# The odd layer's input projection by Strassen's algorithm, with its weight differences made in the even stage

## The chip, the cores and the metric

The kernel runs on one core of a Trainium2 chip. The metric is the device time of one execution in microseconds (us). The engines are PE (TensorE, matmuls), DVE (VectorE), ACT (ScalarE), POOL (GpSimd) and SP (which issues transfers only); each works through its own instructions in order, and each of SP, ACT and POOL can issue transfers.

## The reference

An inference step of a two-layer decoder trunk on a prompt of 2048 tokens and 64 sample tokens (8 sequences of 8), with a model width of 1024, all in fp32. Layer 0 ("even") has one input projection for two mixers: a causal pooling mixer and differential attention. Layer 1 ("odd") is gated linear attention (GLA):

```python
def odd_layer(x, s0, w_in, w_ga, w_gb, b_g, norm_w, w_out, ln_g, ln_b):
    q, k, v, g = jnp.split(x @ w_in, ODD_SPLITS, axis=-1)
    log_a = jax.nn.log_sigmoid(((x @ w_ga) @ w_gb + b_g)) / GLA_TAU
    ...
    o, s_end = gla_chunked(q, k, v, log_a, s0)
    o = rms_norm(o, norm_w).reshape(b, t, ODD_OUT_IN) * jax.nn.silu(g)
    y = layer_norm(DN_ALPHA * x + o @ w_out, ln_g, ln_b)
```

`w_in` of the odd layer has 1024 rows and 3072 columns: q and k with 512 columns each, v and the gate g with 1024 each. The change is about the product `x @ w_in` of this layer.

## The kernel before, in words

**Three products for one.** An fp32 matrix product is made from matmuls in fp32r, a form of lower precision: each operand is split into a high part, rounded, and a low part, the rest (`split`, L40 to L48: the high part by ACT or DVE, the low part on L48 by DVE), and `mm3` (L51 to L56) adds hi x hi, hi x lo and lo x hi in PSUM on three lines. A tensor's tile is 128 partitions wide; "k" counts the eight blocks of 128 of the width.

**Stages.** The even projection goes to about 547 us, attention with its fills to 1215, the odd projection from 1215.3 to 1804.7, and GLA with its output projection from there to the end. A tile scheduler sets the order on each engine from the program and its dependencies; memory that two pools share in turn adds waits (a later pool's tile waits for the last use of what lay there).

**The even projection already runs by Strassen's algorithm, one level**: for each set of 1024 tokens (2 sets) and each group of 1024 weight columns (3 groups), the product of two 2x2 matrices of blocks (x in quarters a11 to a22, weights in quarters b11 to b22, each block 512 x 512) is made of seven block products instead of eight (`fast`). They need sums of x parts (`XParts`, names s1 to s4) and differences of weight quarters (t1 to t4). Only set 0's first group is made plainly. `WParts` makes the differences once on the chip and puts them into DRAM; for the groups 1 and 2 in wide pieces (`make_wide`), for group 0 in pieces of 256 columns with four quarters in the single set of tiles of a pool, `comb`:

```python
with self.tc.issue_after(self.last.ins):
    for x in QUARTERS:
        b.append(pool.tile([128, n], F32, tag=x, name=f"{self.pre}m{x}{g}_{c}"))
        nc.gpsimd.dma_start(b[-1], self.at(g, x)[:, c:c + n])
for x, v in differences(nc, *b).items():
    nc.gpsimd.dma_start(self.t[g][x][:, c:c + n], v)
```

These are four loads (L386), four DVE differences (L336 to L339) and four stores (L388) a piece, all transfers on POOL's queue. The profile calls the tiles pmb and the differences' tensors pt; a wide piece is pn. `run` in `project_even` lets one more piece follow every second step of a product.

**Attention** goes head by head over 16 tiles of 128 tokens: scores (sc, in PSUM), exponentials (e), transposes (tp to aT), the product with the values (po) in the one bank of pool `apso`, and the result oq, which ACT copies from po and which is multiplied with a gate (sga, loaded by SP). oq and sga lie in a pool `arp`, opened once the even projection has closed its pools. `weave` puts fills between: the out projection of the pooling mixer (`out_pool`: products zp, with results zx, stored to z by POOL, and operands zh and zl split from zr by POOL or ACT) beside head 0, the samples' attention beside head 1, and the out projection of attention beside heads 2 and 3.

**The odd projection** (`Odd`, `project_odd`) keeps all its x resident, in hi and lo parts (`XSplit`), in the token chunks `CH` of 512, 512, 512, 256 and 320; the last holds the 64 sample tokens. q and k (products qm) come with weights as the stationary side, by 128 columns and chunk; v and the gate (vt) by tiles of 128 tokens. Each is a plain product: three matmuls for each of eight k. The forget gate (ga, gz, the scan to cb) runs beside q and k. 24 weight units of 128 x 1024 are loaded by SP into a ring of two (raw) and split to wk; v leaves through ACT's queue, q, k and cb through SP's, the gate through POOL's. Beside its last 5 token tiles, GLA's first chunks (`inside`) and four of the eight out weights are got ready; the other four follow, and then SP, DVE and the other engines pass a branch (L1420) that picks one of two forms of GLA. The loads of GLA's gates (gsg, gcb) stand behind it.

Of the kernel before, what the change touches and what calls it, by code (L numbers as in the profile page):

```python
# [26 lines left out]


CH = [(0, 512), (512, 512), (1024, 512), (1536, 256), (1792, 320)]
# [43 lines left out]
class XSplit:  # L73


    def __init__(self, tc, pools, raws, src, pre):
        self.tc, self.pools, self.raws, self.src, self.pre = tc, pools, raws, src, pre
        self.hi, self.lo = {}, {}

    def place(self, c, pool=None):  # L80
        pool = pool or self.pools[c]
        for z, part in (("h", self.hi), ("l", self.lo)):
            part[c] = pool.tile([128, 8, CH[c][1]], F32R, name=f"{self.pre}{z}{c}")

    def load(self, c, pool=None, before=None):

        nc = self.tc.nc
        t0, n = CH[c]
        if c not in self.hi:
            self.place(c, pool)  # L90
        h, l = self.hi[c], self.lo[c]
        for k in range(0, 8, 2):
            if before:
                before(k)
            raw = self.raws[(k // 2) % len(self.raws)]
            r = raw.tile([128, 2, n], F32, tag="raw", name=f"{self.pre}r{c}_{k}")
            load = nc.sync.dma_start(r, self.src[k:k + 2, :, t0:t0 + n].rearrange("k p t -> p k t"))
            split(nc, r, h[:, k:k + 2, :], l[:, k:k + 2, :], "act" if k % 4 or before else "dve")
        return load

    def tok(self, t0, n):
        for c, (c0, cn) in enumerate(CH):
            if c0 <= t0 < c0 + cn:
                o = t0 - c0
                return (lambda k: self.hi[c][:, k, o:o + n]), (lambda k: self.lo[c][:, k, o:o + n])

    def both(self, t, t0, n):

        c, o = next((c, t0 - c0) for c, (c0, cn) in enumerate(CH) if c0 <= t0 < c0 + cn)
        self.tc.nc.vector.tensor_copy(t[:, :, 0:n], self.hi[c][:, :, o:o + n])  # L110
        self.tc.nc.vector.tensor_copy(t[:, :, n:2 * n], self.lo[c][:, :, o:o + n])
        return lambda k: t[:, k, :]


# [32 lines left out]

class XParts:
# [14 lines left out]
    def sums(self, h):  # L163

        nc = self.tc.nc
        for x, y, op, z in (("s3", "a11", ALU.subtract, "a21"), ("s1", "a21", ALU.add, "a22"),
                            ("s2", "s1", ALU.subtract, "a11"), ("s4", "a12", ALU.subtract, "s2")):
            if x == "s1":
# [261 lines left out]
def layers(tc, d):  # L430
# [6 lines left out]
    with ExitStack() as left:  # L437
# [11 lines left out]
        for m, j in project_even(tc, d, dr, W, slot, psf):  # L449
# [26 lines left out]
    with ExitStack() as left:  # L476
# [4 lines left out]
        O = Odd(tc, d, odd, keep, A.ident)  # L481
# [13 lines left out]
    fill_banks.close()  # L495
# [4 lines left out]
def project_even(tc, d, dr, W, slot, psf):  # L500
# [4 lines left out]
    with ExitStack() as own:  # L505
# [7 lines left out]
        P = WParts(tc, dr, d["w0_q"], "p")  # L513
# [832 lines left out]
class Odd:  # L1346


    def __init__(self, tc, d, ctx, keep, ident):
        self.tc, self.d, self.ctx, self.ident = tc, d, ctx, ident  # L1350
# [4 lines left out]
        self.W = Weights(tc, self.raw, self.place, 200)  # L1355

# [3 lines left out]
    def first_weights(self):  # L1360
        self.w_first = [self.W.fm(self.d["w1_fm"][j]) for j in range(2)]

    def start(self):

        self.xq, self.p1 = ExitStack(), ExitStack()
        rq = self.pool(self.xq, "p1rq", 1, side="right")
        self.ps = self.pool(self.p1, "p1ps", 6, space=PSUM)
        self.X = XSplit(self.tc, {}, [self.raw, self.raw, rq], self.d["y0T"], "y")
        for c in range(2):
            self.load_right(c)  # L1370
        self.w_first += [self.W.fm(self.d["w1_fm"][j]) for j in (2, 3)]

    def load_right(self, c):
        self.X.load(c, self.pool(self.xq, f"p1xq{c}", 1, side="right"))

    def run(self):
        tc, d, ctx = self.tc, self.d, self.ctx
        nc = tc.nc
        cst = self.pool(ctx, "p1c", 1)
        ident = self.ident  # L1380
        steep = cst.tile([1, 32], I32, name="steep")[:, 0:1]
        self.load_right(2)
        xp = self.pool(self.p1, "p1x", 1)
        ev = self.pool(self.p1, "p1e", 10)

        def slot(name, n=512, dt=F32):
            return ev.tile([128, 512], dt, tag="g", name=name)[:, :n]

        last = project_odd(tc, d, self, cst, xp, slot, ident, steep)
        self.xq.close()  # L1390

        gw = self.pool(ctx, "gw", 4, side="right")
        gl = self.pool(ctx, "gl", 1, side="right")
        G = Gla(tc, d, ident, self.raw, gl)
        W = Weights(tc, self.raw, places(gw), 300)

        def bank(name):
            return self.ps.tile([128, 512], F32, tag="mm", name=name)

        def early():  # L1400
            for i in range(2):
                G.load(i, G.first + ("v1",))
            for k in range(4):
                G.w.append(W.unit(d["w1_out"][k]))
# [923 lines left out]
```

## Time and profile before

| | us |
|---|---|
| runs | 2173.31, 2176.49, 2186.42; median 2176.49 |
| profiled execution | 2179.26, its span 2177.5 |
| even projection, 0 to 547 | PE busy 525.6 |
| attention and fills, 547 to 1215.3 | 668.3, PE busy 604.9 |
| odd projection, 1215.3 to 1804.7 | 589.4, PE busy 586.9, DVE 165.4, ACT 115.9, POOL 69.8 |
| GLA and output, 1804.7 to 2177.5 | 372.8, PE busy 333.0 |

The mean granted clock of PE was 0.983. A row of instructions in the trace has the start, the duration, the engine, the line, the operation, the tile written and the tiles read, and the shape. In lists by line stand the count, the busy time with the mean in ns, and the idle time of the engine before them with what ended it. Buffer numbers are left out of names.

### The profile page before, as it was taken

The numbers are of one execution on the slowest core, as the hardware profiler recorded it, in microseconds if no ns is written. First come the engines' busy times: TensorE is split into PE (matmuls) and PEld (weight loads), VectorE is DVE, ScalarE is ACT, GpSimd is POOL, SyncE is SP. The second block draws the span as 40 slices with busy tenths as digits, with TensorE's granted clock in tenths as the row PEclk, the third lists the DMA queues.
The fourth block names the chain that finished last, engine by engine and source line by source line (L and its number), as shares of the span: only waits on it lengthen the run. The fifth ranks groups of instructions, "written<-read, shape, count | busy, mean of one in ns | idle before, by whom it ended". The sixth has DMA issues, their size and how long they took to land. (4 is left out here: it accounts for less than half of the span.)

```text
span 2177.5 us, 31247 instructions
## 1 busy us (share of the span) xinstructions
PE 2050.4 (94%) x11153; PEld 1688.1 (78%) x11153; DVE 1337.1 (61%) x2592; ACT 823.9 (38%) x1610; POOL 805.1 (37%) x975
## 2 busy tenths in 40 slices
PE   8999999999999999798888899999999997999997
PEld 7778788877788777587777688888888886778776
DVE  7698665656867666988676554710110127898894
ACT  4245442445533556654645212301111134333341
POOL 2345324125645423766443200000004343645554
PEclk9999999999999999999999999999999998999999
DMA  8877766268855797633322452311221237455422
GB/s 287 285 239 242 240 197 213 82 134 245 271 168 164 223 308 226 212 108 126 102 66 78 148 181 91 120 65 49 85 84 54 97 131 222 155 170 165 171 91 75
DMA packets 201064, 346.71 MB, mean 159 GB/s; under 512 B 26034, under 2 KB 108338, under 8 KB 200898
## 3 DMA queue, kind: packets, MB, share of 16 engines
q1 hardware_dynamic: 143282, 219.96, 32.9%
q0 software_dynamic: 33408, 104.47, 13.6%
q10 hardware_dynamic: 24208, 20.19, 2.8%
q8 instruction: 90, 1.47, 0.3%
q14 instruction: 76, 0.62, 0.1%
HBM read 229.56 MB, written 114.96 MB: 158 GB/s over the span
## 5 line engine op out<-in xcount | busy, mean ns | idle before, releaser
L1561 POOL TENSOR_TENSOR ve<-ve,nw 128x512 f32<-128x512 f32 (+1 forms) x34 | 44.8, 1320 | 473.2 <-ACT ve L1560 473.1
L1069 ACT ACTIVATE e<-sc,nm 128x896 f32<-128x896 f32 (+11 forms) x192 | 165.0, 865 | 121.5 <-DVE nm L1067 82.9
L56 PE MATMUL vt<-wk,yl 128*128 128x512 f32 x512 | 199.9, 391 | 0.0
L55 PE MATMUL vt<-wk,yh 128*128 128x512 f32 x512 | 199.7, 390 | 0.0
L54 PE MATMUL vt<-wk,yh 128*128 128x512 f32 x512 | 197.1, 391 | 0.0
L1054 DVE TENSOR_REDUCE nm<-sc 128x1 f32<-128x768 f32 (+7 forms) x160 | 156.7, 991 | 30.5 <-PE sc L1050 18.3
L48 DVE TENSOR_TENSOR wl<-wr,wh 128x1024 fp32r<-128x1024 f32 (+1 forms) x93 | 112.4, 1213 | 87.8 <-ACT wh L43 87.6
L47 DVE CAST wk<-wr 128x1024 fp32r<-128x1024 f32 x14 | 10.5, 751 | 251.8 <-PE vt L64 250.4
L1049 PE MATMUL sc<-kst,qh 128*128 128x512 f32 (+9 forms) x352 | 134.6, 385 | 29.4 <-ACT e L1069 27.3
L1094 PE MATMUL po<-vt,aT 128*128 128x128 f32 x1088 | 153.1, 280 | 3.5 <-ACT aT L1106 2.1
L1094 PEld LDWEIGHTS po<-vt,aT 128*128 128x128 f32 x1088 | 137.8, 194 | 10.2 <-ACT aT L1106 2.4
L43 ACT ACTIVATE wh<-wr 128x1024 fp32r<-128x1024 f32 (+1 forms) x86 | 88.9, 1038 | 129.2 <-PE f L55 64.2
L1106 ACT ACTIVATE aT<-tp 128x512 f32<-128x512 f32 (+3 forms) x160 | 85.6, 535 | 100.3 <-PE tp L1101 99.8
L1050 PE MATMUL sc<-kst,ql 128*128 128x512 f32 (+9 forms) x352 | 123.0, 352 | 0.0
L54 PE MATMUL qm<-yh,wk 128*128 128x512 f32 (+2 forms) x320 | 113.7, 356 | 5.4 <-DVE yh L47 4.8
L55 PE MATMUL qm<-yl,wk 128*128 128x512 f32 (+2 forms) x320 | 113.9, 356 | 0.0
L56 PE MATMUL qm<-yh,wk 128*128 128x512 f32 (+2 forms) x320 | 113.7, 355 | 0.0
L55 PEld LDWEIGHTS vt<-wk,yh 128*128 128x128 f32 x512 | 96.2, 188 | 20.5
L54 PEld LDWEIGHTS vt<-wk,yh 128*128 128x128 f32 x512 | 96.2, 188 | 20.5
L56 PEld LDWEIGHTS vt<-wk,yl 128*128 128x128 f32 x512 | 96.2, 188 | 20.5
L1049 PEld LDWEIGHTS sc<-kst,qh 128*128 128x128 f32 x352 | 68.3, 194 | 50.0 <-ACT e L1069 39.7
L1101 PE MATMUL tp<-ident,e 128*128 128x128 f32 x544 | 91.3, 282 | 12.8 <-ACT aT L1106 10.2
(646 smaller groups left out, 5799.6 us busy)
## 6 DMA issues: line engine op xcount, KB each, us to landing
wr<-pt SPq DMA_DIRECT2D x40, 512.0 KB, 6.4
wr<-in_w_q SPq DMA_DIRECT2D x37, 512.0 KB, 4.9
sk<-in_cachek SPq DMA_DIRECT2D x64, 256.0 KB, 3.8
sv<-in_cachev SPq DMA_DIRECT2D x64, 256.0 KB, 4.7
pt<-pn POOLq DMA_DIRECT2D x32, 256.0 KB, 7.3
qr<-q SPq DMA_DIRECT2D x64, 128.0 KB, 4.1
kr<-k SPq DMA_DIRECT2D x32, 256.0 KB, 4.2
zx<-in_x SPq DMA_DIRECT2D x32, 256.0 KB, 3.0
```

The lines of the kernel that those rows point to most:

```text
L43: h = nc.scalar.activation(hi, raw, AF.Copy)
L48: return h, (lo_eng or nc.vector).tensor_tensor(out=lo, in0=raw, in1=hi, op=ALU.subtract)
L54: nc.tensor.matmul(ps, lh(k), rh(k), start=(first and k == 0), stop=False, **kw)
L55: nc.tensor.matmul(ps, lh(k), rl(k), start=False, stop=False, **kw)
L56: nc.tensor.matmul(ps, ll(k), rh(k), start=False, stop=(last and k == n - 1), **kw)
L1049: nc.tensor.matmul(o, qh[:, c, qs], kst[:, ks], start=True, stop=False)
L1050: nc.tensor.matmul(o, ql[:, c, qs], kst[:, ks], start=False, stop=k < npc - 1)
L1054: nc.vector.tensor_reduce(out=nm[:, c, i:i + 1], in_=p[:, :, :w], op=ALU.max, axis=AX.XY, negate=True)
L1069: nc.scalar.activation(o, p, AF.Exp, bias=nm[:, m, 0:1], accum_out=s[:, m, i if npc > 1 else 0:][:, :1])
L1094: nc.tensor.matmul(po, s[:, 128 * j:128 * j + 128], vt[:, k0 + j, :], start=(k0 + j == 0), stop=(k0 + j == n - 1))
L1101: nc.tensor.transpose(p[:, 128 * j:128 * j + 128], a[:, 128 * (k0 + j):128 * (k0 + j) + 128], self.ident)
L1106: nc.scalar.activation(s[:, :128 * g], p[:, :128 * g], AF.Copy)
```

## The change

**Even stage.** Two `WParts` are made, P for the even weights and P2 for the odd ones (names rmb and rt in place of pmb and pt, lines L351 and L353). Once P's pieces are out, P2's 24 pieces of 256 columns follow in the same pool `comb`, for the groups 1, 2 and 0.

**Odd projection.** `XSplit` goes, and `project_odd` is written anew in the manner of the even stage: two sets of 1024 tokens by three groups of columns (q and k; v; gate). Set 0's group 0 is plain (`plain_rows`, 8 block products), the other five go through `fast`, with 7 block products of 48 matmuls of 512 columns each. Operand sums are made on DVE while products run, with s2 now written over a21. Weights are no longer resident: two units per block product, 78 in all, go through the same ring of two. The sample tokens go at the side of set 1's products (`side`), two matmuls for a k. Results are copied or added by ACT and DVE, and all their stores go through POOL's queue. The forget gate is made by set, with 96 rows in place of 128.

**Hand-over to GLA.** The early work of GLA is spread over the last block products, with one out weight; the other seven come behind them, four into the places of the projection's weights.

The core of the diff:

```diff
-        for m, j in project_even(tc, d, dr, W, slot, psf):
+        P, P2 = (WParts(tc, dr, d[f"w{i}_q"], "pr"[i]) for i in range(2))
+        for m, j in project_even(tc, d, P, P2, W, slot, psf):
...
             yield from P.make(comb, (0,))
+
+            P2.last = P.last
+            yield from P2.make(comb, (1, 2, 0))
...
-        for k in range(4, 8):
-            G.w.append(W.unit(d["w1_out"][k]))
+        self.p1.close()
+        self.fill_banks.close()
+        gw = places(self.pool(ctx, "gw", 3, side="right"))
+        for k in range(1, 8):
+            self.out_weights(G, k, gw if k > 4 else self.place)
         G.buf["s"] = [self.raw.tile([128, 1024], F32, tag="raw", name=f"gs_{i}") for i in range(2)]
-        self.p1.close()
-        r = nc.values_load(steep[0:1, 0:1], min_val=0, max_val=1)
+        r = nc.values_load(self.steep[0:1, 0:1], min_val=0, max_val=1)
...
+    X.room.update(zip(("s3", "s1", "s4"), left))
+    sums = X.sums(0, "s2")
...
+    run(plain_rows(X, nc, first_weights, bank, queries_keys(0, False)), first_parts(), wait=8)
+    O.few.close()
+    O.ev = O.pool(O.p1, "p1e", 8)
+    run(fast(nc, X, weights(1), False, bank, qbank, place, values(0)), sums)
+    nw = norm_weights(0)
...
+    run(fast(nc, X, weights(2), False, bank, qbank, place, out_gates(0, nw)), next_parts())
...
+    run(fast(nc, X, weights(0), True, bank, qbank, place, queries_keys(1, True),
+             scale=lambda j: 128 ** -0.5, side=side(sample_queries_keys, "ya")), last_parts(), wait=0)
...
+    run(fast(nc, X, weights(1), False, bank, qbank, place, values(1), side=side(sample_values, "yb")), second_gates(),
+        wait=8)
     lowest()
+    nw = norm_weights(1)
+    for m, j in fast(nc, X, weights(2), False, bank, qbank, place, out_gates(1, nw), side=side(sample_gates(nw), "yc")):
+        yield m, j
```

`fast` itself is not changed; its inner loop is

```python
for m in order:
    wm = w(PARTS[m][1])
    if side:
        side(m, wm, True)
    for j in range(4):
        open_(m, j)
    for u in (0, 2):
        for j in range(4):
            for k in (u, u + 1):
                mul(m, j, wm, k)
            if u:
                done(m, j)
                yield m, j
```

**How instructions move.** First POOL's queue at the start of attention (head 0). zx are results of the pooling mixer's out projection, stored to z; zh and zl its next operands; s1q, sga and oq belong to attention. Before, in a row:

```order
L1132 TENSOR_TENSOR oq4_0_4954<-oq4_0_4954,sga0_2_4670 128x256
L1137 DMA mixa_62<-oq4_0_4954 128x2x128
L1224 DMA z0_63<-zx0_0_4534 128x512
L1224 DMA z0_63<-zx0_1_4535 128x512
L1224 DMA z0_63<-zx1_0_4757 128x512
L45 TENSOR_SCALAR zh3_5023<-zr3_5017 128x512
L1224 DMA z0_63<-zx1_1_4758 128x512
L48 TENSOR_TENSOR zl3_5024<-zr3_5017,zh3_5023 128x512
```

And now, in a row:

```order
L1191 DMA z0_63<-zx2_1_5307 128x512
L351 DMA rmb110_512_2615<-in_w1_q 128x256
L351 DMA rmb120_512_2617<-in_w1_q 128x256
L351 DMA rmb220_512_2621<-in_w1_q 128x256
L351 DMA rmb210_512_2619<-in_w1_q 128x256
L45 TENSOR_TENSOR zl3_5420<-zr3_5413,zh3_5419 128x512
L42 TENSOR_SCALAR zh4_5527<-zr4_5521 128x512
L353 DMA rt10_98<-rmb110_512_2615 128x256
L353 DMA rt30_100<-rmb120_512_2617 128x256
L45 TENSOR_TENSOR zl4_5528<-zr4_5521,zh4_5527 128x512
L353 DMA rt20_99<-rmb220_512_2621 128x256
L353 DMA rt40_101<-rmb210_512_2619 128x256
```

The last eight pieces of the odd weights (group 0, columns 0 to 1792 in steps of 256) stand here, mixed with the stores and splits of zp's run, and attention's oq and mixa have moved behind all of them.

On PE in the same place, before (e are exponentials, aT transposed ones, vt values):

```order
L1101 MATMUL tp6_0_4_5110<-ident_4213,e6_0_0_4885 128x128 x3
L1094 MATMUL po6_0_5081<-vt0_4570,aT6_0_0_5087 128x128 x4
L54 MATMUL zp0_0_4604<-wh79_4539,zh0_4600 128x512
L54 MATMUL zp0_1_4691<-wh79_4539,zh0_4600 128x512
L1094 MATMUL po6_0_5081<-vt0_4570,aT6_0_4_5114 128x128 x3
L1101 MATMUL tp7_0_0_5201<-ident_4213,e7_0_0_4972 128x128 x4
L55 MATMUL zp0_0_4604<-wl79_4540,zh0_4600 128x512
```

And now, at the end of zp's run:

```order
L53 MATMUL zp11_1_6366<-wh81_4948,zl11_6329 128x512
L51 MATMUL zp11_1_6366<-wh82_4958,zh11_6328 128x512
L1061 MATMUL po1_0_5081<-vt0_4966,aT1_0_0_5085 128x128 x2
L52 MATMUL zp11_1_6366<-wl82_4959,zh11_6328 128x512
L53 MATMUL zp11_1_6366<-wh82_4958,zl11_6329 128x512
```

po1, the second tile of head 0, stands behind 286 rows of zp that follow one another without a break from the first half of sc8; before, po6 was done when zp began.

Last, DVE's queue before its branch to GLA, before (wk are split out weights, gkl and gatt GLA's first chunk, ve a result of the projection):

```order
L48 TENSOR_TENSOR gkl_1_16360<-gkp1_16517,gkh_1_16358 128x512
L1705 COPY_PREDICATED gatt1_16370<-gmk_16367,gap1_16536 128x512
L48 TENSOR_TENSOR wk307_16612<-wr307_16611,wk307_16612 128x1024
L47 CAST wk308_16617<-wr308_16616 128x1024
L70 TENSOR_TENSOR ve3_16_16594<-vt3_16_16488,vs3_16595 64x512
L48 TENSOR_TENSOR wk308_16617<-wr308_16616,wk308_16617 128x1024
L1419 TENSOR_LOAD steep_12889
L1420 COMPARE_AND_BRANCH
```

And now (u are results of the last block product, nw the norm's weights):

```order
L1550 TENSOR_TENSOR u2_16786<-u2_16786,nw1_16554 128x512
L45 TENSOR_TENSOR wk304_17244<-wr304_17243,wk304_17244 128x1024
L1550 TENSOR_TENSOR u3_16794<-u3_16794,nw1_16554 128x512
L44 CAST wh306_17254<-wr306_17253 128x1024
L45 TENSOR_TENSOR wl306_17255<-wr306_17253,wh306_17254 128x1024
L45 TENSOR_TENSOR wl307_17261<-wr307_17259,wh307_17260 128x1024
L44 CAST wh308_17266<-wr308_17265 128x1024
L45 TENSOR_TENSOR wl308_17267<-wr308_17265,wh308_17266 128x1024
L1372 TENSOR_LOAD steep_13326
L1373 COMPARE_AND_BRANCH
```

The splits of three more out weights now stand between the last results (u3) and the branch.

More of the change, by code (lines that the diff above doesn't have):

```diff
@@ L1378, in run @@
         nc = tc.nc
[L1379 to L1403, printed above, removed]
-                G.w.append(W.unit(d["w1_out"][k]))
-                yield 800
-                if k == 1:
-                    yield from G.inside(0, 1, True, bank)
-                    G.two("a", G.R[0], "att", "dve")
-                elif k == 3:
-                    yield from G.inside(1, 1, True, bank)
-                    G.two("v", G.R[0], "v1", "act")
@@ new lines, in early, with bank @@
+    def early(self, G, gw):
+        def bank(name):
+            return self.psf.tile([128, 512], F32, tag="f", name=name)
+        for i in range(2):
+            G.load(i, G.first + ("v1",))
+        yield
+        for i in range(2):
+            for _ in G.inside(i, 1, True, bank):
+                yield
+            if i:
+                G.two("v", G.R[0], "v1", "act")
+            else:
+                G.two("a", G.R[0], "att", "dve")
+                self.out_weights(G, 0, places(gw))
+            yield
@@ new lines, in sample_gates, with f, side, place_ @@
+    def sample_gates(nw):
+        def f(z, o):
+            nc.scalar.activation(o, o, AF.Silu)
+            nc.vector.tensor_tensor(out=o, in0=o, in1=nw[:NS, 512 * z:512 * z + 512], op=ALU.mult)
+            nc.gpsimd.dma_start(d["sg1"][NP:T, 512 * z:512 * z + 512], o)
+        return f
+    def side(done, name):
+        def place_(n):
+            return cst.tile([128, 512], F32, tag="se", name=n)
+        return SampleSide(nc, x_s, qbank, place_, slot, done, name)
+    def run(gen, then=(), wait=4):
+        then = iter(then)
+        for i, _ in enumerate(gen):
+            if later:
+                later.pop(0)()
+            if i >= wait:
+                next(then, None)
```

381 lines of the change are left out of this document (202 added, 179 removed).

## The prediction

> **What bounds the kernel now.** I read the page first: busy time, then the slices.
>
> ```profile
> span 2177.5 us, 31247 instructions
> PE 2050.4 (94%) x11153; PEld 1688.1 (78%) x11153; DVE 1337.1 (61%) x2592; ACT 823.9 (38%) x1610; POOL 805.1 (37%) x975
> PE   8999999999999999798888899999999997999997
> ```
>
> PE is the bound almost everywhere, so the question is how many matmul columns go, and where PE will have to wait anew. Next, busy time by windows (window, its length, then busy us of PE, PEld, DVE, ACT, POOL, the granted clock, the DMA share, GB/s): one window of the odd projection, then stretches of the even one, which already runs by Strassen.
>
> ```profile
> 1500.00:1510.00 10.00, 10.00 (x45) 8.15 (x44) 0.00 (x0) 1.20 (x2) 0.00 (x0) 1.00 0.14 52
> 100.00:125.00 25.00, 20.84 (x90) 16.28 (x89) 24.11 (x46) 8.84 (x15) 15.51 (x28) 1.00 0.96 354
> 125.00:150.00 25.00, 24.21 (x107) 19.62 (x106) 24.51 (x44) 14.53 (x22) 9.23 (x17) 1.00 0.59 190
> 200.00:225.00 25.00, 22.96 (x102) 18.64 (x100) 15.11 (x25) 10.17 (x16) 12.91 (x24) 1.00 0.88 291
> 225.00:250.00 25.00, 24.28 (x93) 19.52 (x94) 16.57 (x23) 11.46 (x18) 5.53 (x11) 0.86 0.58 190
> 300.00:325.00 25.00, 25.00 (x113) 20.38 (x113) 17.78 (x26) 12.46 (x19) 1.64 (x3) 1.00 0.45 140
> 525.00:550.00 25.00, 20.80 (x93) 15.61 (x92) 20.25 (x27) 14.63 (x31) 22.64 (x29) 0.99 0.91 285
> ```
>
> The odd projection lets PE wait for nothing; columns removed there come off the end one for one. Strassen's schedule can also keep PE full (300 to 325), but not where weight differences are made (100 to 250) nor at the hand-over to attention (525).
>
> **The change part by part.**
>
> *Matmuls.* The order of PE counts, from the last matmul of attention to the first of GLA's output, 2284 of 512 columns, 212 of 320 and 212 of 256 before; now 2296 of 512 and 28 of 64 (the samples' gates and transposes). The start-to-start times stand in PE's timeline of the odd projection:
>
> ```profile
> 1399.66 0.39 PE L56 MATMUL qm<-yh,wk 128*128 128x512 f32 x1
> 1409.86 0.39 PE L56 MATMUL qm<-yh,wk 128*128 128x512 f32 x1
> 1295.78 0.31 PE L55 MATMUL qm<-yl,wk 128*128 128x320 f32 x1
> 1301.20 0.31 PE L56 MATMUL qm<-yh,wk 128*128 128x320 f32 x1
> 1315.73 0.28 PE L56 MATMUL qm<-yh,wk 128*128 128x256 f32 x1
> 1317.89 0.28 PE L56 MATMUL qm<-yh,wk 128*128 128x256 f32 x1
> ```
>
> Over 45, 37 and 18 steps that is 0.227, 0.147 and 0.120 us. Saved: 212 x 0.147 + 212 x 0.120 = 56.6; given back: 12 x 0.227 = 2.7 and, for the 28 small ones at about 0.08 (an estimate below the 256-column row), 2.2. **−51.7 us.** Strassen saves an eighth of the products in five of six blocks, yet the number of wide matmuls stays: what goes is the narrow tail, because the 64 sample rows now ride at the side.
>
> *Differences of the odd weights.* They are 24 more pieces of 128x256 quarters, each four loads, four VectorE differences and four stores on POOL's queue. The eight such pieces of the even weights show the price: issues on POOL by line, their starts on VectorE (first, three in the middle, last), and the median landing of load and store.
>
> ```profile
> L388 POOL DMA_DIRECT2D pt<-pmb x32 | 17.4, 547 | 37.4 <-DVE pmb L338 13.1 <-DVE pmb L337 9.8 <-DVE pmb L336 7.2
> L386 POOL DMA_DIRECT2D pmb<-in_w_q x32 | 17.3, 542 | 20.9 <-DMA pt<-pmb 18.9 <-DMA out_newkT<-ro 1.7 <-issue 0.2
> 153.12 0.42 DVE L336 TENSOR_TENSOR pmb<-pmb,pmb 128x256 f32<-128x256 f32 x1 [1.27 <-DMA pmb<-in_w_q]
> 163.36 0.43 DVE L336 TENSOR_TENSOR pmb<-pmb,pmb 128x256 f32<-128x256 f32 x1 [1.49 <-DMA pmb<-in_w_q]
> 173.54 0.43 DVE L336 TENSOR_TENSOR pmb<-pmb,pmb 128x256 f32<-128x256 f32 x1 [0.27 <-DMA pmb<-in_w_q]
> L386 POOL DMA_DIRECT2D pmb<-in_w_q x32: 538/543/568, 109.5 to 216.0; - x32
> L388 POOL DMA_DIRECT2D pt<-pmb x32: 542/547/590, 126.3 to 236.9; - x32
> pmb<-in_w_q POOLq DMA_DIRECT2D x32, 128.0 KB, 4.3
> pt<-pmb POOLq DMA_DIRECT2D x32, 128.0 KB, 3.4
> ```
>
> With one set of four tiles the pieces are a chain: four issues (4 x 0.54), landing 4.3, two last differences 0.84, an issue, landing 3.4 makes 11.2 us; measured, 10.2 undisturbed, and (236.9 − 109.5)/8 = 15.9 in the mean. The mean is what the chain costs when POOL and VectorE have other things ahead of it.
>
> In the even stage sixteen of the 24 pieces run beside products that do not need them. What they can delay is the second set's x parts, whose loads now stand between pieces on POOL's queue. The four windows shown between 100 and 250 lost 4.16 + 0.79 + 2.04 + 0.72 = 7.7 us with eight pieces; as much per piece makes 15.4 for sixteen; hidden entirely, 0 (a gain is excluded: nothing leaves this stage). VectorE was full in the first two of those windows and is at 17.8 of 25 from 300: nearer the lower end. **+6** (0 to 15).
>
> The last eight pieces are the main point. Their four tiles lie where attention keeps its results and gates (oq, sga), so the first result of head 0 cannot be written before the last of these stores has landed, and the orders of ACT and SP hold that wait. There is one bank for po, so the second output tile of attention stands behind it, and PE's order shows what runs meanwhile: 286 rows of the pooling mixer's out projection (zp), pulled together from where they lay between scores.
>
> ```profile
> L54 PE MATMUL zp<-wh,zh x128: 387/393/483, 570.6 to 709.7; 128*128 128x512 f32 x128
> 700.00:725.00 25.00, 23.98 (x152) 20.33 (x151) 15.76 (x34) 8.86 (x24) 14.82 (x25) 1.00 0.65 180
> ```
>
> These cover 286 x 0.227 = 64.9 us. Against them stand seven pieces (the eighth is done before the run starts). At 10.2 they take 71 us, and a lead of 2 and a tail of 5 (landing 3.4, the result's copy, the next product) make 78: 13 us of waiting. But POOL's own queue puts two stores of z, a zh and a zl between pieces, which are not all in the chain's waits: I take 11.5 a piece, nearer the undisturbed rows, since only these few stand between: 80 + 7 − 65 = 22. At 15.9 it is 111 + 7 − 65 = 53. Later softmax waits also lack the fill used up early; the window from 700, where zp is running out, loses 1.0 of 25, and five such windows are 5 to 6. **+28** (0 if the pieces keep ahead of zp, 60 at 15.9).
>
> The two rows of landings can be set beside a rule. The Trainium skill ("DMA: Bandwidth & Descriptors", section "Anatomy of one DMA — SWDGE (gpsimd) path") fits a GpSimd-issued transfer at 2.0 us plus a nanosecond for each 436 bytes, an estimated 2.3 us for these 128 KB; the chain would then be 8.2 us and the block gone, which is the first rival below. The trace's 4.3 and 3.4 us and 10.2 per piece do not agree, so the sum goes by the rows.
>
> *The odd stage itself.* The operands' sums, splits and results now go to VectorE and ACT, and weights are streamed in 78 units instead of 24 resident ones. The same code in the even stage, hand-over aside, lost the 7.7 us above; VectorE's load per block is up to 95 of 96 us in the plain one by my count of its instructions (0.68 per 512 columns), some 40 to 64 of 76 in the others. A stream that keeps up costs 0; those losses with the hand-over's 4.2 (the window at 525) are 12. **+5** (0 to 12).
>
> *Hand-over to GLA.* Before, four out weights were loaded early. Now seven wait for the last product's places, and VectorE's and SP's branch stands behind them. The rows of this transition and of one weight:
>
> ```profile
> 1815.00:1820.00 5.00, 1.56 (x5) 0.97 (x5) 1.22 (x7) 0.40 (x1) 1.05 (x1) 0.50 1.07 346
> 1804.53 0.40 PE L64 MATMUL vt<-wk,ys 128*128 128x512 f32 x1
> 1808.64 1.75 DVE L48 TENSOR_TENSOR gql<-ge,gqh 128x512 fp32r<-128x512 f32 x1
> 1821.37 0.78 DVE L1814 SCALAR_TENSOR_TENSOR gm<-go,rmofg,gsg 128x256 f32<-128x256 f32 x2
> wr<-in_w_out SPq DMA_DIRECT2D x14, 512.0 KB, 3.7
> L48 DVE TENSOR_TENSOR wl<-wr,wh 128x1024 fp32r<-128x1024 f32 (+1 forms) x93 | 112.4, 1213 | 87.8 <-ACT wh L43 87.6
> L43 ACT ACTIVATE wh<-wr 128x1024 fp32r<-128x1024 f32 (+1 forms) x86 | 88.9, 1038 | 129.2 <-PE f L55 64.2
> ```
>
> PE issues its last projection matmul at 1804.5 and goes on at 1804.7 (T), VectorE is past the branch at T+4, and gm at T+16.7 lets the output start. Now a staging ring of two forces pairs: the fifth weight's load at about T+3.5, landed and split (3.7 + 1.04 + 1.21) at T+9.4, when the last pair starts and SP may branch; that pair is split by T+9.4 + 3.7 + 1.04 + 2 x 1.21 = T+16.6, about when VectorE branches. The gates' loads, issued after SP's branch, come some 7 us later than before. **+7** (0 if they are not what is waited for, 12 if VectorE's 12.6 us come through whole).
>
> *Sum* for the profiled execution: 2177.5 − 51.7 + 6 + 28 + 5 + 7 = 2171.8 span. Its own time was 1.8 above its span and 2.8 above the median of the runs, so I forecast **2170.8 us**, 0.3% less.
>
> **The rivals.**
>
> *The gain arrives nearly whole.* The pieces keep ahead of zp (9 us each or less) and everything else hides: losses 0 + 5 + 3 + 5 = 13, giving 2176.5 − 51.7 + 13 = 2138 us. For it: the undisturbed 10.2 is not far from 9, and PE was full in most windows of the even stage. Against: the chain's own rows add to 11.2, with nothing left to overlap.
>
> *Slower: the pieces go at the mean of before.* If POOL is as disturbed at the start of attention as from 109 to 237, a piece takes 15.9, attention waits 60 and the even stage 15: 2176.5 − 51.7 + 60 + 15 + 5 + 7 = 2212 us. With 15 in the even stage it is over 1% slower from 14.1 us a piece; with 6 there it eats the gain from about 12.2. For it: the windows at 525 have POOL busy 22.64 of 25 and DMA at 0.91, and 25 MB more are moved. Against: in the middle rows the chain kept 10.2 while VectorE was full.
>
> *The weight stream limits the odd stage.* A product of 48 matmuls is 48 x 0.227 = 10.9 us and needs two units.
>
> ```profile
> wr<-in_w_q SPq DMA_DIRECT2D x37, 512.0 KB, 4.9
> ```
>
> By that row, 4.9 + 1.04 + 1.21 = 7.2 per pair; landing must pass 8.6 us before PE waits. At 2 us late for each of 39 products the time is 2250. Against: the same stream fed the window from 300 without a wait.
>
> **How the numbers follow.** Forecast 0.52, nearly whole 0.27, slower by pieces 0.17, weight stream 0.04. A measurement of this kernel can tell about 1%, that is 2154.7 and 2198.3. Faster: 0.27 and 0.07 of the forecast's lower side, 0.34. Slower: 0.14 of the pieces' case, 0.04, and 0.02 of the forecast's upper side, 0.20. The likeliest case by itself, with pieces from 10 to 13 us, is 2155 to 2190; the range for eight in ten reaches to both neighbours, 2138 to 2212.
>
> **What would show it.** Right: the odd projection about 52 us shorter and PE full in it but for a few us; between head 0's first scores and its second po, one run of zp with POOL issuing rmb pieces some 11 us apart, and about 20 us of PE waiting on them; ACT's first oq waiting for an rt store; GLA's first gm some 23 us after the last projection matmul. Wrong: zp spread between the scores as before; pieces done before attention starts; PE waiting inside the odd blocks for weights (wk) or for operand sums; or the narrow matmuls' time not coming off.

## The result, and the profile after

The changed kernel takes **2234.28 us** (median of 4 runs, 2232.70 to 2243.62) against 2179.97 before (4 runs): a ratio of 1.0258, 95% interval [1.0214, 1.0303]. It is 2.6% slower. The forecast was 2170.8, the range ended at 2212, and slower had a chance of 0.20.

The page of the changed kernel, first lines and the slices of PE and of its granted clock:

```profile
span 2232.3 us, 31671 instructions
## 1 busy us (share of the span) xinstructions
PE 2042.4 (91%) x10769; PEld 1658.7 (74%) x10769; DVE 1525.8 (68%) x2905; ACT 976.7 (44%) x1809; POOL 918.9 (41%) x1257
...
PE   8999998989689999779888989999999896999987
...
PEclk9999999998899999899998999999999997999999
```

PE is busy only 8 us less, where the count of matmuls took some 50 off, and the span is 55 us longer: PE idles 62.8 us more, and a part of its busy time is slower matmuls. The slices name the place: the low digits from the 11th slice on, which is 558 to 700 us, where before stood nines. Four windows of that stretch, and attention as a whole before and after, with the odd projection last (window, length, busy us of PE, PEld, DVE, ACT, POOL, granted clock, DMA share, GB/s; the first row is of the kernel before):

```profile
547.00:1215.30 668.30, 604.94 (x4274) 497.99 (x4274) 494.06 (x1088) 349.14 (x787) 343.67 (x427) 0.98 0.54 168
```

```profile
575.00:600.00 25.00, 17.06 (x61) 12.77 (x62) 18.17 (x32) 6.18 (x10) 12.01 (x15) 0.73 0.80 208
600.00:625.00 25.00, 16.60 (x57) 12.03 (x56) 9.38 (x13) 2.94 (x5) 17.83 (x25) 0.80 0.94 297
625.00:650.00 25.00, 19.58 (x79) 14.23 (x79) 9.23 (x14) 0.00 (x0) 20.22 (x34) 1.00 0.85 288
650.00:675.00 25.00, 20.06 (x70) 14.02 (x69) 7.46 (x14) 0.00 (x0) 17.65 (x30) 0.88 0.75 245
559.00:1311.20 752.20, 647.50 (x4314) 524.37 (x4314) 516.27 (x1139) 358.23 (x802) 378.50 (x497) 0.94 0.54 168
1311.20:1854.80 543.60, 532.98 (x2354) 434.95 (x2353) 310.00 (x460) 263.74 (x373) 91.43 (x161) 0.99 0.48 161
```

ACT does nothing at all from 625 to 675: it stands at one instruction. ACT's own waits from 575 to 700 say which, and the rows of attention's first and last result (oq, first and last start) of the kernel before and of the changed one say what it did to the stage:

```profile
ACT oq L1088 <- DMA rt<-rmb: 72.7, 1, 72.7
```

```profile
L1121 ACT ACTIVATE oq<-po x64: 261/277/309, 553.2 to 1210.5; 128x128 f32<-128x128 f32 x64
```

```profile
L1088 ACT ACTIVATE oq<-po x64: 254/277/322, 681.4 to 1296.2; 128x128 f32<-128x128 f32 x64
```

The first result waits 72.7 us for the last store of the odd weights' pieces and comes 128 us late; at the last result 85.7 us of it are left. From there the stages count as follows.

| profiled execution, us | before | after | difference |
|---|---|---|---|
| last result of attention | 1210.5 | 1296.2 | +85.7 |
| from it to PE's last projection matmul | 594.2 | 558.5 | −35.7 |
| from there to GLA's first gm | 16.7 | 22.9 | +6.2 |
| gm to the end | 356.1 | 354.7 | −1.4 |
| sum (span) | 2177.5 | 2232.3 | +54.8 |

So the projection did become shorter, and the price of making its weight differences was more than twice what it saved.

### The profile page after: what moved, and what is told of

Its sections match the earlier page's. It is cut to its first block, busy times and chain, and to the rows that moved or that the text cites. A ratio compares the mean times of both kernels' runs of the same rounds, so it can differ in the third digit from the quotient of the medians.

```text
span 2232.3 us, 31671 instructions
## 1 busy us (share of the span) xinstructions
PE 2042.4 (91%) x10769; PEld 1658.7 (74%) x10769; DVE 1525.8 (68%) x2905; ACT 976.7 (44%) x1809; POOL 918.9 (41%) x1257
## 3 DMA queue, kind: packets, MB, share of 16 engines
q0 software_dynamic: 52192, 160.59, 20.3%
## 5 line engine op out<-in xcount | busy, mean ns | idle before, releaser
L45 DVE TENSOR_TENSOR wk<-wr,wk 128x1024 fp32r<-128x1024 f32 x82 | 100.1, 1223 | 109.8 <-ACT wk L40 109.7
L40 ACT ACTIVATE wk<-wr 128x1024 fp32r<-128x1024 f32 x78 | 82.2, 1057 | 123.4 <-PE f L53 95.5
L1016 PEld LDWEIGHTS sc<-kst,qh 128*128 128x128 f32 x352 | 71.3, 203 | 67.5 <-ACT e L1036 54.4
L1045 DVE SCALAR_TENSOR_TENSOR e<-e,c,e 128x128 f32<-128x128 f32 (+15 forms) x64 | 94.5, 1477 | 1.2
L1068 PEld LDWEIGHTS tp<-ident,e 128*128 128x128 f32 x544 | 66.5, 149 | 31.3 <-ACT aT L1073 18.0
L353 POOL DMA_DIRECT2D rt<-rmb x96 | 52.5, 549 | 75.9 <-DVE rmb L301 24.8
L1088 ACT ACTIVATE oq<-po 128x128 f32<-128x128 f32 x64 | 17.7, 276 | 146.3 <-DMA rt<-rmb 72.7
L1017 PEld LDWEIGHTS sc<-kst,ql 128*128 128x128 f32 x352 | 71.7, 204 | 3.3
L1039 DVE TENSOR_TENSOR s<-s 128x1 f32<-128x1 f32 x64 | 24.4, 381 | 66.1 <-ACT e L1036 65.7
L51 PE MATMUL zp<-wh,zh 128*128 128x512 f32 x128 | 54.9, 430 | 12.1 <-DVE zx L1188 5.8
L351 POOL DMA_DIRECT2D rmb<-in_w_q x96 | 52.7, 550 | 20.5 <-DMA rt<-rmb 15.8
```

What stands on the lines that cost most here:

```text
L40: h = nc.scalar.activation(hi, raw, AF.Copy)
L45: return h, (lo_eng or nc.vector).tensor_tensor(out=lo, in0=raw, in1=hi, op=ALU.subtract)
L51: nc.tensor.matmul(ps, lh(k), rh(k), start=(first and k == 0), stop=False, **kw)
L1016: nc.tensor.matmul(o, qh[:, c, qs], kst[:, ks], start=True, stop=False)
L1017: nc.tensor.matmul(o, ql[:, c, qs], kst[:, ks], start=False, stop=k < npc - 1)
L1045: nc.vector.scalar_tensor_tensor(out=es[0][:, :nk], in0=es[1][:, :nk], scalar=c2, in1=es[0][:, :nk], op0=ALU.mult, op1=ALU.add)
```

## The experiments

Two theories stood at first. "Place": attention lost its time because its results lie in the memory of the last eight pieces. "Traffic": the pieces cost it by their work beside attention, wherever results lie. A third, that the new odd projection is to blame, had to be tried too. Ratios are to the kernel before on the same chip (median 2179.0 for the first four, 2179.8 for the next three and the last, 2178.8, 2182.2 and 2176.7 for the three in between).

**Results elsewhere.**

```diff
+        self.vts.append(self.pool("avt1", 1, side="right"))
         self.rp = self.pool("arp", 2, side="right")
         self.e.insert(0, self.pool("ae4", 1, side="right"))
-        self.vts.append(self.pool("avt1", 1, side="right"))
```

> Only the order in which attention opens two pools is changed, so that the tiles of oq and sga lie 8 KB lower and head 1's values lie where the pieces' four tiles were. All 24 pieces stay. Theory 'place' (attention lost its 83 us because its first result had to wait for the memory of the last pieces): oq's first copy at about 570 us, zp spread over the scores, time about 2160 us (2150 to 2175). Rival 'traffic' (the pieces cost that time by their POOL and DMA work beside attention, wherever results lie): within 15 us of 2234.

Measured: 2206.42 us, 1.0129 [1.0106, 1.0153]. Neither theory as it stood: 27.9 us come back, where "place" alone would have brought some 75 and "traffic" alone under 15. The rows of oq, and windows of the same stretch:

```profile
L1088 ACT ACTIVATE oq<-po x64: 257/278/305, 570.9 to 1270.6; 128x128 f32<-128x128 f32 x64
```

```profile
559.00:575.00 16.00, 7.79 (x32) 5.75 (x31) 8.04 (x11) 2.75 (x6) 9.61 (x16) 0.84 1.01 352
575.00:600.00 25.00, 20.09 (x81) 15.44 (x82) 22.69 (x43) 14.72 (x35) 14.80 (x21) 0.69 1.02 267
600.00:680.00 80.00, 74.80 (x455) 63.89 (x454) 63.41 (x137) 35.38 (x80) 56.51 (x93) 1.00 0.60 195
```

The 128 us at the first result are gone (17.7 are left, of the even stage), yet at the last one 60 stand: PE waits 8.2 and 4.9 us before 600, at a clock of 0.84 and 0.69, and 5.2 more to 680; the rest is lost behind.

**Without the late pieces.**

```diff
-            yield from P2.make(comb, (1, 2, 0))
+            yield from P2.make(comb, (1, 2))
+            P2.t[0] = P2.t[1]
```

> Leaves out the last eight pieces (group 0 of the odd weights); the second set's q and k are computed with group 1's differences in their place, which changes their values and no instruction. Both theories: about 2155 us (2145 to 2165), the even stage's 13 us staying with the 16 other pieces. What tells them apart is the distance to the kernel with results elsewhere: 'place' under 10 us, 'traffic' over 40.

Measured: 2166.81 us, 0.9943 [0.9921, 0.9966], 39.6 below the kernel with results elsewhere. The time lies just outside the 2145 to 2165 that was expected, and the distance just under the 40 that was asked of 'traffic'. The stretch from 600 to 680 is full again, and attention's last result comes at 1226.4:

```profile
600.00:680.00 80.00, 80.00 (x425) 68.06 (x424) 57.17 (x99) 28.43 (x61) 44.77 (x64) 1.00 0.66 204
```

So the eight late pieces cost 67.5 us: 27.9 by their place and 39.6 that stay when results lie elsewhere. Both theories hold a part. Most of the 39.6 is lost late: the kernel with results elsewhere is 10.6 us behind this one at the first result of head 1 (772.0 against 761.4), and 44.5 at the first of head 2 (959.8 against 915.3), although its last piece is out by 727. The split assumes that the new order of pools costs nothing by itself. Head 1's values now lie where the pieces were, and in head 1 PE waits for no load of them; but no run has that order without the late pieces.

**Without any pieces.**

```diff
-            P2.last = P.last
-            yield from P2.make(comb, (1, 2, 0))
+            P2.t = P.t
```

> Leaves out all 24 pieces; the odd projection reads the even weights' differences instead, which changes values and no other instruction. Both theories: the even stage and attention as before the change, the odd projection 46 us shorter, the hand-over 6 longer: about 2140 us (2132 to 2150). If a part of the loss has another cause than the pieces (the odd stage's own code), it stays over 2160.

Measured: 2146.79 us, 0.9847 [0.9824, 0.9870]. The sixteen early pieces cost 20.0 us, all 24 together 87.5. What is left of Strassen without its differences is a gain of 32 us and not 40: its attention ends where it did before, at 1212.4, and the stretch to the last projection matmul is 33.6 us shorter, near the 35.7 of the changed kernel.

```profile
L1087 ACT ACTIVATE oq<-po x64: 257/277/295, 554.1 to 1212.4; 128x128 f32<-128x128 f32 x64
```

**The kernel before, with the pieces.**

```diff
         P = WParts(tc, dr, d["w0_q"], "p")
+        P2 = WParts(tc, dr, d["w1_q"], "r")
...
             yield from P.make(comb, (0,))
+
+            P2.last = P.last
+            yield from P2.make(comb, (1, 2, 0))
```

> The kernel before with the 24 pieces made in the even stage and nothing else; their results are not used. 'Place' and 'traffic': before + 13 + 83, about 2275 us (2260 to 2285), with one unbroken run of zp. If the loss comes from the new odd projection or its early loads instead: under 2200 us.

Measured: 2267.65 us, 1.0410 [1.0385, 1.0436]: +88.6 us without any Strassen in the odd layer, the 87.5 of the test above from the other side. This loss belongs to the pieces and needs nothing of the new odd projection. That the odd projection gains less than was worked out is another matter, and smaller.

**What of the work it is.** Bytes and DVE time, or the queue. From the kernel with results elsewhere, the last eight pieces are cut to 32 columns:

```diff
-    def make(self, pool, groups, n=256):
+    def make(self, pool, groups, n=256, only=256):
...
-                        nc.gpsimd.dma_start(b[-1], self.at(g, x)[:, c:c + n])
-                for x, v in differences(nc, *b).items():
-                    nc.gpsimd.dma_start(self.t[g][x][:, c:c + n], v)
+                        nc.gpsimd.dma_start(b[-1][:, :only], self.at(g, x)[:, c:c + only])
+                for x, v in differences(nc, *(z[:, :only] for z in b)).items():
+                    nc.gpsimd.dma_start(self.t[g][x][:, c:c + only], v)
...
-            yield from P2.make(comb, (1, 2, 0))
+            yield from P2.make(comb, (1, 2))
+            yield from P2.make(comb, (0,), only=32)
+            P2.t[0] = P2.t[1]
```

> The kernel with results elsewhere (2206 us), the last eight pieces cut to 32 of 256 columns: as many loads, differences and stores on the same queues, an eighth of the bytes and little DVE time; the second set's q and k use group 1's differences, values changed. That kernel stands 40 us above the one without the late pieces (2167 us). Theory 'POOL queue' (64 transfers to issue, 35 us, and the waits at their head delay attention's own POOL work): stays at 2190 to 2206 us. Rival 'bytes and DVE': falls to within 10 us of 2167.

Measured: 2206.85 us, 1.0126 [1.0095, 1.0157], the same as with whole pieces (2206.42), although an eighth of the bytes moved and a difference takes 0.19 us in place of 0.42. The landings of whole and narrow pieces, and the late pieces' rows on POOL and DVE:

```profile
rmb<-in_w_q POOLq DMA_DIRECT2D x64, 128.0 KB, 4.6
rmb<-in_w_q POOLq DMA_DIRECT2D x32, 16.0 KB, 2.5
```

```profile
L353 POOL DMA_DIRECT2D rt<-rmb x28: 538/558/617, 593.2 to 718.0; - x28
L301 DVE TENSOR_TENSOR rmb<-rmb,rmb x7: 178/186/883, 589.6 to 712.0; 128x32 f32<-128x32 f32 x7
```

Bytes and the length of DVE's work are ruled out. What did not change is the number of entries on the in-order queues: 64 transfers on POOL, 0.54 to 0.56 us each whatever their size, some 35 us, with what waits at their head, between zp's zh, zl and stores to z and attention's own s1q, ql, oq and mixa. It fits that zp falls behind: some 107 of its 400 matmuls run after the first result of head 1 (744.0), none in the kernel without the late pieces. So by elimination the 40 us lie with these entries. How they divide into issue time, waits at the head, DVE's 32 short entries, the new order of pools and the order that the scheduler made around the pieces was not separated.

**Group 0's pieces in the odd stage.** If the queue is the price, the pieces belong where POOL has nothing urgent: the odd projection's second block.

```diff
-            yield from P2.make(comb, (1, 2, 0))
+            yield from P2.make(comb, (1, 2))
...
+    def pieces(g, quarters):
+        for c in range(0, 2048, 256):
+            b = quarters(f"rm{g}_{c}")
+            for x, v in zip(QUARTERS, b):
+                nc.gpsimd.dma_start(v, P.at(g, x)[:, c:c + 256])
+            for x, v in differences(nc, *b).items():
+                nc.gpsimd.dma_start(P.t[g][x][:, c:c + 256], v)
+            yield ""
...
-    run(fast(nc, X, weights(1), False, bank, qbank, place, values(0)), sums)
+    run(fast(nc, X, weights(1), False, bank, qbank, place, values(0)), beside(sums, pieces(0, one)))
```

(`one` gives four quarters of the tile `shared`, `two_slots` below two scratch slots of `slot`; `beside` takes a piece after each step of the other work, and `either` below takes the two places in turn.)

> The eight pieces of group 0 are made during the odd projection's second block, where POOL is idle, in a place shared with the gate's weights; the other 16 as in the change. Nothing left out. 'Place' and 'POOL queue': the time without late pieces, 2167 us, within 6, since POOL has 13 of 76 us of work there; a rival, that the pieces cost 35 to 40 us beside any stage: 2200 us.

Measured: 2167.64 us, 0.9953 [0.9930, 0.9977]; that is the 2166.81 without late pieces within the noise, so eight pieces cost nothing there that can be told. This is the one complete kernel that beats both: 0.5% faster than before and 66.6 us faster than the change.

**Two groups in the odd stage**, to save the early pieces' 20 us as well:

```diff
-            yield from P2.make(comb, (1, 2))
+            yield from P2.make(comb, (1,))
...
-... beside(sums, pieces(0, one)))
+... beside(sums, pieces(2, one)))
-... out_gates(0, nw)), next_parts())
+... out_gates(0, nw)), beside(next_parts(), pieces(0, two_slots)))
```

> Of the 24 pieces eight (group 1) stay in the even stage, group 2's are made in the odd projection's second block and group 0's in its third. Nothing left out. If the 16 pieces in the even stage cost 20 us in proportion, this gives about 2157 us (2150 to 2163); if the first eight cost nothing there, 2147; if DVE in the third block (44 to 64 of 76 us busy) cannot take the pieces, over 2167.

Measured: 2199.92 us, 1.0084 [1.0054, 1.0115]; a miss. Attention's last result came 7 us earlier than with 16 early pieces, at 1221.4, but the odd stage lost more, in one wait of PE for a weight whose difference was not stored yet:

```profile
PE f L51 <- ACT wk L40: 30.2, 2, 27.1
```

Three mends of it followed, each aimed at the wait that the one before had shown.

*Two sets of tiles:* group 2's pieces alternate between `one` and `two_slots`.

```diff
-... pieces(2, one)))
+... pieces(2, either)))
```

> As the kernel with two groups in the odd stage (2200 us), but group 2's pieces alternate between the shared place and two scratch slots, so that a piece need not wait for the stores of the one before. Nothing left out. In that kernel PE waited 27 us at the start of the odd projection's third block for weights that were not stored yet, and ran at half clock after it. Theory 'the chain of one set of tiles was too long for one block': that wait goes, and the time is about 2160 us (2152 to 2168). Rival 'the scratch slots and DVE are too full in the third block': stays over 2185.

Measured: 2194.13, 1.0072 [1.0047, 1.0097], as the rival said. The 27 us are gone, and in their place stand 15.5 us until ACT has copied results (se) that stand in its queue behind the splits of s2, and 13.2 us for the samples' operand (ys). The loads for both were queued behind pieces:

```profile
PE f L51 <- ACT se L1549: 15.5, 1, 15.5
PE yax L273 <- DVE ys L45: 13.2, 1, 13.2
```

*Parts first:* group 0's pieces start only behind the loads of a11, a12 and s2.

```diff
-... beside(next_parts(), pieces(0, two_slots)))
+... beside(next_parts(), pieces(0, two_slots), 12))
```

> As the kernel with two sets of tiles (2194 us), but in the odd projection's third block group 0's pieces are issued only behind the loads of the second set's first operands (a11, a12 and s2). There PE waited 15.5 and 13.2 us for work on these operands, whose loads stood behind pieces on POOL's queue. Theory 'whatever stands behind a piece in POOL's queue is late': those two waits go, 2158 us (2150 to 2168). Rival 'DVE and slots in the third block are too full': the waits move to other products, over 2180.

Measured: 2201.18, 1.0084 [1.0063, 1.0106]; no better, and again the rival's side. The 15.5 us are gone, but the samples' operand is now behind all of the pieces, and its wait has grown from 13.2 to 34.3:

```profile
PE yax L273 <- DVE ys L45: 34.3, 1, 34.3
```

*Samples first:* the four lines that load and split the samples' operand move ahead of the third block.

```diff
     nw = norm_weights(0)
+    x_s = cst.tile([128, 8, 128], F32R, name="ys16")
+    xr = slot("ysr").rearrange("p (k t) -> p k t", k=8)
+    nc.gpsimd.dma_start(xr, d["y0T"][:, :, NP:T].rearrange("k p t -> p k t"))
+    split(nc, xr, x_s[:, :, :NS], x_s[:, :, NS:])
```

> As the kernel with the parts first (2201 us), but the load and split of the samples' operand (ys) are put ahead of the third block too. There PE waited 34.3 us for that split, which stood behind the pieces on POOL's and DVE's queues, as the only long wait of that block. Theory 'whatever stands behind a piece in a queue is late, and nothing else': the wait goes, 2160 us (2150 to 2168). Rival 'the third block has no room': a wait of over 15 us turns up at the next operand (s3, s1 or the differences rt themselves), over 2180.

Measured: 2184.50, 1.0036 [1.0018, 1.0054]. That wait went too, and the rival's came: 17.3 us for a weight, with the last of group 0's pieces stored at 1539.7, when PE stood waiting from 1533. In the third block the pieces have no room that costs nothing. PE's wait, and the pieces' stores (first and last start):

```profile
PE f L51 <- ACT wk L40: 19.8, 3, 17.3
```

```profile
L1618 POOL DMA_DIRECT2D rt<-rm x64: 539/540/547, 1332.7 to 1539.7; - x64
```

**Fewer late out weights**, from the kernel with group 0 in the odd stage, for the hand-over to GLA:

```diff
-            self.out_weights(G, k, gw if k > 4 else self.place)
+            if k > 4:
+                G.w.append(G.w[k - 4])
+            else:
+                self.out_weights(G, k, self.place)
```

> The kernel with group 0 in the odd stage, three of the seven late out weights (the fifth to seventh) not loaded and split; the first three stand in for them, values changed. Theory 'the late weights hold up the branch' as in the prediction: 5 to 8 us less than with them. Rival 'the gates' loads or the results of the last block are what GLA waits for': within 2 us.

Measured: 2159.75 us, 0.9907 [0.9878, 0.9936], 7.9 below its base. DVE's first instruction behind the branch comes 5.3 us after PE's last projection matmul (1785.2 to 1790.5) and not 14.7 (1788.7 to 1803.4), the first gm at 17.9 and not 23.2. Some 3 us of the 7.9 had been gained by the end of attention, where this edit changes nothing, so 5 are the weights'. The rows of the kernel with fewer:

```profile
1785.00 0.39 PE L53 MATMUL f<-wk,ys4l 128*128 128x512 f32 x1
...
1790.48 0.68 DVE L45 TENSOR_TENSOR gql<-ge,gqh 128x512 fp32r<-128x512 f32 x1
1803.10 1.66 DVE L1925 SCALAR_TENSOR_TENSOR gm<-go,rmofg,gsg 128x256 f32<-128x256 f32 x4 [0.28 <-POOL rmofg L2316]
```

## Why the prediction was wrong, point by point

**The matmuls (−51.7): right, within 3 us.** In the odd projection PE's busy time is 533.0 for 543.6 us of stage, where before it was 586.9 for 589.4, that is 53.9 less. Some 5 of these are 24 of the last 48 matmuls of attention's out projection, which now run ahead of the stage; the other 48 to 49 are the narrow tail, 3 short of the count.

**The late pieces (+28, 0 to 60): the step that failed.** The mechanism was named: ACT's oq waits for the last rt store, zp runs in one piece, po1 comes behind it. But the term measured 67.5 us. In the block itself it was near, with 27 us of idle PE from 575 to 700 against 22 worked out. Three things in the working were wrong.

First, the cover was taken whole: 286 zp matmuls as 64.9 us of work against the chain. But zp's operands zh and zl and its stores to z stand in the same POOL queue as the pieces, so PE could run zp only as fast as POOL got through both. PE's waits for POOL from 575 to 700:

```profile
PE zp L53 <- POOL zl L45: 7.2, 5, 2.8
PE zp L51 <- POOL zh L42: 5.6, 1, 5.6
```

POOL at the start of the block, and then the loads of one piece after another:

```profile
583.33 2.19 POOL L351 DMA_DIRECT2D rmb<-in_w_q  x4
593.37 1.29 POOL L45 TENSOR_TENSOR ql<-qr,qh 128x512 fp32r<-128x512 f32 x1 [7.86 <-ACT qh L40]
594.88 1.25 POOL L1191 DMA_DIRECT2D z<-zx  x2 [0.22 <-issue]
602.23 1.49 POOL L969 TENSOR_TENSOR kst<-kr,kst 64x512 fp32r<-64x512 f32 x1 [6.10 <-ACT kst L967]
...
605.48 0.56 POOL L353 DMA_DIRECT2D rt<-rmb  x1
...
613.10 1.62 POOL L351 DMA_DIRECT2D rmb<-in_w_q  x3
...
624.68 1.07 POOL L351 DMA_DIRECT2D rmb<-in_w_q  x2
...
670.41 1.13 POOL L351 DMA_DIRECT2D rmb<-in_w_q  x2 [1.27 <-DMA rt<-rmb]
```

From 613.1 to 670.4 five pieces take 11.5 us each, exactly the cycle that was forecast. The first takes 30: its stores stand behind a ql and kst that wait 7.9 and 6.1 us for ACT. The chain is 98 us long (583.3 to 681.4) and not 87.

Second, the end of the block was taken for the end of the loss. When zp was used up, head 0 was not left without a fill: from 700 to the first result of head 1, at 828.7, PE idles only 5.3 us, because 264 of the 576 matmuls spo of the samples' attention came forward from head 1. Head 1 then lacks them. Here is attention up to the first result of head 1, and from there to the first of head 2, of the changed kernel and then of the kernel without the late pieces:

```profile
559.00:828.70 269.70, 234.19 (x1502) 179.01 (x1501) 159.65 (x357) 92.91 (x221) 143.59 (x228) 0.94 0.76 239
828.70:980.30 151.60, 127.56 (x1072) 102.09 (x1070) 108.10 (x254) 86.45 (x202) 65.29 (x89) 0.91 0.57 177
```

```profile
559.00:761.40 202.40, 192.41 (x1074) 160.32 (x1072) 137.31 (x277) 83.93 (x186) 112.66 (x157) 0.97 0.65 195
761.40:915.30 153.90, 144.32 (x1524) 112.97 (x1524) 113.26 (x302) 95.51 (x241) 67.18 (x100) 0.99 0.82 262
```

PE idles 35.5 and 24.0 us against 10.0 and 9.6, each at a lower clock; the allowance of 5 us for what comes behind the block, read from one window, was far too small. That the missing fill makes head 1 idle is argued, not shown: with results elsewhere PE idles 22.9 us there with all 576 at hand. Against the kernel before, attention is 83.9 us longer. PE's idle time in it grew from 63.4 to 104.7 us, of which only 27 lie between 575 and 700, and its busy time by 42.6, of which some 5 are the 24 matmuls above. Most of the other busy time is slower matmuls: the granted clock in the two rows of attention above is 0.98 and 0.94, so 668 x 0.02 = 13 and 752 x 0.06 = 45 us are lost, an estimated 32 us more. That is an upper estimate, since the clock is also low while PE idles. The prediction had no term for the clock at all, though its own fence showed 0.50 at a transition. The Trainium skill ("TensorE: Matmul & The Clock Gate", section "Part 1: The HAM clock gate") says that an idle window of about 3.4 us halves PE's clock until it has been busy as long. The trace agrees in part: from 612 to 622, behind a wait of 5.6 us, the clock is 0.54, but it is 0.50 from 577 to 583 too, and no wait from 560 to 577 was over 1.2 us.

Third, only the place was priced. With results elsewhere the pieces still cost 39.6 us, which the test with narrow pieces leaves to their entries on the queues. The prediction's question was whether the pieces keep ahead of zp; it never asked whose work they hold up when they do.

**The early pieces (+6, 0 to 15): mis-sized.** They cost 20.0. The upper bound took the loss per piece from windows in which PE idled and left out the clock and the later start of attention: in the kernel without late pieces PE idles 33.0 of the first 559 us at a clock of 0.98, without any pieces 20.3 of the first 547 at 0.99, and attention's first result comes at 573.2 and 554.1.

**The odd stage (+5, 0 to 12): mis-sized.** From the last result of attention to the last projection matmul it is 35.7 us shorter in the profile, not 46.7. Within the stage PE idles 10.6 us against 2.5 before, the longest wait where the second set's forget gates need gM from DVE; and the first product starts 15.1 us after the last result instead of 4.8.

```profile
PE yby L273 <- DVE gM L1491: 4.4, 1, 4.4
PE f L51 <- ACT wk L40: 2.5, 2, 1.9
PE f L52 <- DVE wk L45: 1.9, 1, 1.9
```

The weight stream is not the bound: its waits are these few us, and that rival fell.

**The hand-over (+7): the size right, the path another.** gm comes 22.9 us after the last projection matmul (1854.7 to 1877.6), against 23.7 worked out. But the 7 us were to come from the gates' loads, and SP issues the first of them (gsg) 8.4 us behind that matmul where before it was 6.0, only 2.4 later. What moved is DVE. It passes the branch 14.4 us behind the matmul and not 4, and is full from there to gm but for 0.3 us, where before it stood 3.8 us for a gate's load (DVE's first row behind the branch now, and that wait before):

```profile
1869.14 0.69 DVE L45 TENSOR_TENSOR gql<-ge,gqh 128x512 fp32r<-128x512 f32 x1
```

```profile
1819.67 0.42 DVE L1673 TENSOR_TENSOR gf<-gcb 128x256 f32<-128x256 f32 x1 [3.78 <-DMA gcb<-cb]
```

That the size came out is partly luck; that the late weights hold up the branch, the test with fewer of them bears out.

With the measured sizes the sum is −51.7 + 20 + 67.5 + 16 + 6 − 1 = +57, and +54.3 was measured. **The rivals:** slower by the pieces had the right place and the wrong mechanism, since six of the seven pieces went at 11 to 11.5 us and not at 15.9; only the first took longer. By the fit of the Trainium skill ("DMA: Bandwidth & Descriptors", section "Anatomy of one DMA — SWDGE (gpsimd) path") that would have made the block vanish, the pieces should have cycled in an estimated 8.2 us. The rows say 11.5.

## What to carry to other kernels

Work that fits into an idle engine's time can still cost much of its length (here 67.5 of the 98 us of the chain): an in-order queue holds up everything behind each waiting entry, so price a background task by whose work stands behind it on each queue, and then by its bytes. A fill covers a wait less than its length says if the fill's own operands come through the queue that is blocked; and what has been used up early is not there to cover later waits, though no run here shows the price of that alone. Put such work in the stage where its queue has nothing urgent: here that took the cost of the same eight pieces from 67.5 us to none that can be told. One block further on, where operands of the next set stand on the same queue, there was no such room.

## What the runs showed of the hardware

A transfer issued by POOL holds its queue 0.54 to 0.56 us for 16 KB as for 128 KB, while the landing falls from 4.6 (the early pieces of that kernel) to 2.5 us. Cutting the bytes to an eighth changed the kernel's time by 0.4 us, which is nothing.

In attention the changed kernel loses 41 us more by PE's idle time and at most an estimated 32 us more by the lower granted clock. Some of the clock is lost in windows in which PE looks full: in the prediction's row from 225 to 250 PE is busy 24.28 of 25 us at a clock of 0.86.
